# Modulation vectors of a two-layer transformer: sixteen sections as narrow matmuls in four column groups instead of elementwise products with sums

## The chip, the cores and the metric

The kernel runs on one core of a Trainium2 chip. The metric is the device time of one execution in microseconds (us). A core has five engines with their own instruction queues: TensorE (PE in the profile, its weight loads PEld), VectorE (DVE), ScalarE (ACT), GpSimd (POOL) and SyncE (SP), which here issues most of the transfers. They meet only at semaphores.

## What is computed

Two layers over 512 latent and 256 context tokens of 1024 features, in float32. Each layer is a feed-forward block, a mixer and a second feed-forward block, each with a residual and a layer norm; the mixer of layer 0 is a gated linear attention with pooling, that of layer 1 differential attention. Every block's input and residual are modulated by vectors made of two condition vectors, one for the latents and one for the context. The change is in how these are made:

```python
c_act = jax.nn.silu(c)
cc_act = jax.nn.silu(c_ctx)
for layer in range(DEPTH):
    m_lat = jnp.split((c_act @ w_ada[layer] + b_ada[layer])[:, None, :], N_MOD, axis=-1)
    m_ctx = jnp.split(cc_act @ w_ada[layer] + b_ada[layer], N_MOD, axis=-1)
    x = ffn_substep(x, m_lat[0:3], w_ffn_in[layer, 0], ...)
    ...
def ffn_substep(x, mods, w_in, w_out, g, b):
    shift, scale, gate = mods
    y = swiglu(modulate(x, shift, scale), w_in, w_out)
    return layer_norm(ALPHA * x + MACARON * gate * y, g, b)
```

So there are 9 sections of 1024 features a layer, 18 in all, and a section is two row vectors times a matrix of 1024 x 1024 (4 MB).

## The kernel before

Features lie on the 128 partitions in 8 blocks, tokens along the free dimension. Products are made in float32r from a high and a low part (`split`, L115 and L117), with three matmuls for one product (`mm3`, L154 to L156). The order of each engine's instructions is set by the framework's scheduler from the program's order and its own costs, so a piece of code can land among its neighbours.

A feed-forward block, `ffn(l, p)`, makes 22 blocks of the hidden layer (`HB`), each from a block of the gate's weights and one of the value's. The first three blocks (`plain`) are made directly (`project`). The other nineteen, numbers 3 to 21, go by seven products of quarter matrices in place of eight (`seven`): 7 x 4 x 3 = 84 matmuls of 384 columns a block, with weight sums on GpSimd (`ahead`, L645 to L654), seven additions on VectorE (L668) and the hidden values written by `put`. The first 512 tokens' hidden values stay on chip (`G`, in the pool `spare` of eleven tiles); the last 256 tokens' are stored to DRAM (late_g, L561, on the SP queue). Then `out_phase` makes the output product in two halves of the tokens, each over eleven pairs of hidden blocks, and `layer_norm` follows.

The modulation is made in three places. `start` makes the first two sections on TensorE: the conditions are the stationary operand (`ct`, 32 columns a step, two of them used), the weights the moving one, and two column groups of the array take the two halves of 1024 columns side by side, one matmul each (L237). `ada` makes the other sixteen within the first three feed-forward blocks: a step of it is called after every `seven`, for the sections of `in_ada`, and after every step of the output product's first half, for those of `out_ada`. A step loads [128 features x 1024 inputs] of the transposed weights (L174) and multiplies by a condition that was broadcast to all partitions (`load_c`, L167), summing along the row:

```python
for v in vecs:
    if v == LAT or j % 2:
        nc.vector.scalar_tensor_tensor(out=self.tmp("trash").bitcast(BF16), in0=r, scalar=1.0,
                                       in1=self.c_bc[v], op0=ALU.mult, op1=ALU.mult, accum_out=col(v))
    else:
        nc.gpsimd.tensor_mul(out=r, in0=r, in1=self.c_bc[v])
        nc.scalar.activation(out=r, in_=r, func=AF.Copy, accum_out=col(v))
```

That is VectorE's line L183 (its output is the tile "trash") and GpSimd's L186 with ScalarE's L187. Three sections lie in each of these stages of the first and second feed-forward block, (0,0) and (0,1), for both vectors; two in each of the third, (1,0), for the latents alone. `mod[l][v]` holds the results as columns.

## Time and profile before

| | |
|---|---|
| time of one execution, median of 3 runs | 2876.92 us (2876.66 to 2877.67) |
| span of the profiled execution, first to last instruction | 2874.1 us |
| mean granted TensorE clock | 0.983 |
| TensorE busy | 2685.2 us (93%) |
| VectorE busy | 2185.1 us (76%) |
| GpSimd busy | 1074.6 us (37%) |
| ScalarE busy | 1237.0 us (43%) |

The profiled execution is told by its span alone; the times of the runs also hold what lies around the span, and their median is 2.8 us above it. Busy shares are means over stages with different limits, so a stage is read by itself: its length, and which engine has no idle time in it. A busy TensorE is one with a matmul under way, and its ends are modelled; what counts is the distance from one matmul's start to the next.

### The profile page before, as it was taken

The page shows a single profiled execution, that of the slowest core. Times are in us where ns is not written, and L with a number is a line of the kernel's source. Part 1 is how long each engine was busy: PE and PEld are TensorE (multiplying, and loading weights), DVE is VectorE, ACT ScalarE, POOL GpSimd, SP SyncE. Part 2 cuts the span into 40 slices and gives each one's busy share as a digit, 9 for nine tenths or more (in the row PEclk, how much of TensorE's full clock was granted, in tenths as well). Part 3 has the DMA queues.
Part 4 walks back from the last instruction along what each step waited for, and adds up shares of the span by engine and source line. Part 5 has one row for each costly group of instructions (what it writes and reads, how often), then busy time and mean ns, then how long its engine had stood idle before and what let it go on. Part 6 is the DMA issues. An engine that isn't in the chain of part 4 may idle for free.

```text
span 2874.1 us, 44394 instructions
## 1 busy us (share of the span) xinstructions
PE 2685.2 (93%) x17168; PEld 2449.1 (85%) x17168; DVE 2185.1 (76%) x3131; ACT 1237.0 (43%) x1919; POOL 1074.6 (37%) x762
## 2 busy tenths in 40 slices
PE   7889999999999888999999899999999998999997
PEld 4789998887877778989788899998987777999997
DVE  3999978765774689997977888664745887778856
ACT  2333333544543343333345433332534667544444
POOL 0655522241220465643334644410424332366402
PEclk9999999999999999999999999999999999999998
DMA  5343255542114223334555333254541101423454
GB/s 221 111 147 112 105 174 207 195 152 67 56 37 152 88 96 139 118 119 139 206 200 180 110 134 119 82 189 165 184 149 59 41 34 45 158 92 122 155 192 157
DMA packets 139671, 374.24 MB, mean 130 GB/s; under 512 B 16962, under 2 KB 48066, under 8 KB 139460
## 3 DMA queue, kind: packets, MB, share of 16 engines
q1 hardware_dynamic: 136832, 370.21, 37.3%
q8 instruction: 135, 2.21, 0.3%
q10 hardware_dynamic: 2628, 1.20, 0.2%
q14 instruction: 76, 0.62, 0.1%
HBM read 337.78 MB, written 33.56 MB: 129 GB/s over the span
## 4 chain that ended last, share of the span: by engine, by line
PE 58%; DVE 22%; issue 7%; ACT 5%; POOL 4%; DMA 3%; SPq 0%; DVEq 0%; POOLq 0%; ACTq 0%
PE ps L156 17%; PE ps L154 17%; PE ps L155 17%; DVE r4l L117 3%; DVE trash L183 3%; DVE c L668 2%; DVE spare L556 1%; DMA raw<-in_w_ffn_out 1%; PE ps L1187 1%; PE ps L1188 1%; PE ps L1189 1%; DVE sm L1089 1%; DVE b L621 1%; ACT r4h L115 1%; DVE late_g L560 1%
## 5 line engine op out<-in xcount | busy, mean ns | idle before, releaser
L117 DVE TENSOR_TENSOR r4l<-raw,r4h 128x1024 fp32r<-128x1024 f32 (+1 forms) x350 | 449.5, 1286 | 215.5 <-ACT r4h L115 176.3
L154 PE MATMUL ps<-xh,r4h 128*128 128x384 f32 (+2 forms) x1672 | 562.5, 337 | 16.6 <-ACT xh L115 7.0
L155 PE MATMUL ps<-xl,r4h 128*128 128x384 f32 (+2 forms) x1672 | 559.1, 335 | 4.8 <-DVE xl L117 3.2
L156 PE MATMUL ps<-xh,r4l 128*128 128x384 f32 (+2 forms) x1672 | 559.0, 335 | 0.0
L115 ACT CAST r4h<-raw 128x1024 fp32r<-128x1024 f32 (+1 forms) x366 | 358.7, 982 | 443.2 <-PE ps L155 330.7
L156 PE MATMUL ps<-six,r4l 128*128 128x384 f32 (+1 forms) x888 | 294.7, 332 | 69.5 <-DVE r4l L117 69.5
L154 PEld LDWEIGHTS ps<-xh,r4h 128*128 128x128 f32 x1672 | 315.1, 189 | 39.7 <-ACT xh L115 9.5
L155 PEld LDWEIGHTS ps<-xl,r4h 128*128 128x128 f32 x1672 | 315.4, 189 | 24.8 <-DVE xl L117 4.9
L156 PEld LDWEIGHTS ps<-xh,r4l 128*128 128x128 f32 x1672 | 315.4, 189 | 18.1
L668 DVE TENSOR_TENSOR c<-c,ps 128x384 f32<-128x384 f32 (+1 forms) x518 | 261.8, 518 | 49.4 <-PE ps L156 39.5
L154 PE MATMUL ps<-six,r4h 128*128 128x384 f32 (+1 forms) x888 | 292.6, 330 | 0.0
L155 PE MATMUL ps<-six,r4h 128*128 128x384 f32 (+1 forms) x888 | 291.4, 328 | 0.0
L156 PE MATMUL ps<-r4h,r4l 128*128 128x512 f32 (+1 forms) x768 | 278.5, 363 | 13.7 <-DVE r4l L117 13.7
L154 PE MATMUL ps<-r4h 128*128 128x512 f32 (+1 forms) x768 | 278.6, 363 | 0.0
L155 PE MATMUL ps<-r4l,r4h 128*128 128x512 f32 (+1 forms) x768 | 277.3, 361 | 0.0
L156 PE MATMUL ps<-r4h,spare 128*128 128x256 f32 (+1 forms) x896 | 261.0, 292 | 11.5 <-DVE spare L117 11.5
L154 PE MATMUL ps<-r4h,spare 128*128 128x256 f32 (+1 forms) x896 | 263.6, 294 | 1.5 <-ACT spare L115 1.5
L155 PE MATMUL ps<-r4l,spare 128*128 128x256 f32 (+1 forms) x896 | 260.6, 291 | 0.1
L156 PEld LDWEIGHTS ps<-six,r4l 128*128 128x128 f32 x888 | 170.8, 192 | 77.6 <-DVE r4l L117 77.6
L645 POOL TENSOR_TENSOR late<-raw 128x512 f32<-128x512 f32 x74 | 116.6, 1575 | 255.1 <-DMA raw<-in_w_ffn_in 219.2
L654 POOL TENSOR_TENSOR raw<-raw,late 128x512 f32<-128x512 f32 x74 | 98.2, 1327 | 251.3 <-DVE r4l L117 233.8
L156 PEld LDWEIGHTS ps<-r4h,spare 128*128 128x128 f32 x896 | 172.8, 193 | 16.3 <-DVE spare L117 14.2
(292 smaller groups left out, 5969.8 us busy)
## 6 DMA issues: line engine op xcount, KB each, us to landing
raw<-in_w_ffn_in SPq DMA_DIRECT2D x176, 512.0 KB, 4.0
raw<-in_w_ffn_out SPq DMA_DIRECT2D x176, 512.0 KB, 4.2
spare<-in_w_ada SPq DMA_DIRECT2D x80, 512.0 KB, 5.0
six<-in_w_ada SPq DMA_DIRECT2D x64, 512.0 KB, 5.3
g<-late_g SPq DMA_DIRECT2D x88, 128.0 KB, 2.2
raw<-g SPq DMA_DIRECT2D x44, 256.0 KB, 3.3
raw<-in_w_in_even SPq DMA_DIRECT2D x20, 512.0 KB, 3.4
raw<-in_w_in_odd SPq DMA_DIRECT2D x16, 512.0 KB, 3.3
```

The costliest lines, as they stand in the source:

```text
L115: self.copied = self.nc.scalar.copy(out=h, in_=src)
L117: eng.tensor_sub(out=l, in0=src, in1=h.bitcast(F32))
L154: mm(out=ps, lhsT=h, rhs=xh, start=first, stop=False)
L155: mm(out=ps, lhsT=h, rhs=xl, start=False, stop=False)
L156: mm(out=ps, lhsT=l, rhs=xh, start=False, stop=last)
L183: nc.vector.scalar_tensor_tensor(out=self.tmp("trash").bitcast(BF16), in0=r, scalar=1.0, in1=self.c_bc[v], op0=ALU.mult, op1=ALU.mult, acc ...
L556: nc.vector.tensor_mul(out=G(x)[:, 0, a:e], in0=gate[:, :e - a], in1=up[:, :e - a])
L560: nc.vector.tensor_mul(out=t, in0=gate[:, o:b - a], in1=up[:, o:b - a])
L621: sub = lambda o, a, b: nc.vector.tensor_sub(out=o, in0=a, in1=b)
L645: nc.gpsimd.tensor_add(out=s1, in0=a21, in1=a22)
L654: nc.gpsimd.tensor_sub(out=a12, in0=a12, in1=sums[:, 512:])
L668: add = lambda o, a, b: nc.vector.tensor_add(out=o, in0=a, in1=b)
```

## The change

The sixteen sections go to TensorE as well, in pairs. One step takes 128 of the 1024 inputs of both sections: two loads of 512 KB and four matmuls, each of 32 stationary columns (`conditions(k)`, two of them used) and 512 moving ones, for four column groups of the array, whose sums lie in one bank of PSUM on 32 partitions each. After eight steps ScalarE copies the bank, TensorE transposes it in four pieces, and VectorE adds the bias into `mod`. 8 pairs x 8 steps = 64 steps. All of them lie within the seven products of the first three feed-forward blocks, spread over ten calls behind hidden blocks 3 to 12 (24, 24 and 16 steps); the output product has none any more. The weights are loaded in their own order and no longer transposed. The broadcast of the conditions and its copy in DRAM are gone. `ct` is one tile of 46 columns, in which step k's 32 columns begin at 2k, so its transfer writes 64 bytes in one run on each partition, where it wrote 8 runs of 8 bytes. Two small tiles of `_lower_bound` are reused. Docstrings and comments are removed throughout; these lines are left out here.

```diff
-        self.ct = self.tmp("ct")[:, :KB * 32].rearrange("p (k c) -> p k c", k=KB)
+        self.ct = c.tile([P, 2 * KB + 30], F32, name="ct")
         nc.vector.memset(self.ct, 0.0)
-        nc.scalar.dma_start(out=self.ct[:, :, 0:2], in_=ins["ct"])
+        nc.scalar.dma_start(out=self.ct[:, :2 * KB].rearrange("p (k c) -> p k c", k=KB), in_=ins["ct"])
...
-    def load_c(self, tiles):
...
-            nc.sync.dma_start(out=t, in_=(self.ins["c"] if first else self.c_act)[v, :].partition_broadcast(P))
...
-    def ada_load(self, room, l, s, j):
...
-    def ada_block(self, r, l, s, j, vecs):
...
-            if v == LAT or j % 2:
-                nc.vector.scalar_tensor_tensor(out=self.tmp("trash").bitcast(BF16), in0=r, scalar=1.0,
-                                               in1=self.c_bc[v], op0=ALU.mult, op1=ALU.mult, accum_out=col(v))
-            else:
-                nc.gpsimd.tensor_mul(out=r, in0=r, in1=self.c_bc[v])
-                nc.scalar.activation(out=r, in_=r, func=AF.Copy, accum_out=col(v))
...
-    def ada(self, sections, tiles, room, steps):
...
+    def conditions(self, k):
+        return self.ct[:, 2 * k:2 * k + 32]
+
+    def ada(self, sections, room, calls):
+        nc = self.nc
+        pairs = [sections[i:i + 2] for i in range(0, len(sections), 2)]
+        steps = [(q, k) for q in range(len(pairs)) for k in range(KB)]
+        def load(q, k):
+            r = [room() for _ in range(2)]
+            for t, (l, s) in zip(r, pairs[q]):
+                nc.sync.dma_start(out=t, in_=self.ins["w_ada"][l, s, k])
+            return r
+        ahead = [load(*steps[0])]
+        for i, (q, k) in enumerate(steps):
+            if i + 1 < len(steps):
+                ahead.append(load(*steps[i + 1]))
+            if k == 0:
+                ps = self.ps("st")
+            for g, (r, c) in enumerate(itertools.product(ahead.pop(0), range(2))):
+                nc.tensor.matmul(out=ps[32 * g:32 * g + 32, :], lhsT=self.conditions(k), rhs=r[:, c * 512:c * 512 + 512],
+                                 start=k == 0, stop=k == KB - 1)
+            if k == KB - 1:
+                self.ada_finish(pairs[q], ps)
+            if (i + 1) * calls // len(steps) > i * calls // len(steps):
+                yield
+
+    def ada_finish(self, pair, ps):
+        nc = self.nc
+        m = self.tmp("m")
+        nc.scalar.copy(out=m, in_=ps)
+        pt = self.ps()
+        for t in range(4):
+            nc.tensor.transpose(out=pt[:, t * P:(t + 1) * P], in_=m[:, t * P:(t + 1) * P], identity=self.ident)
+        pv = pt.rearrange("p (t i c r) -> p i c t r", t=4, i=2, c=2)
...
+            for v in (LAT, CTX) if l == 0 or s < 5 else (LAT,):
+                o = self.mod[l][v][:, s * KB:(s + 1) * KB]
+                nc.vector.tensor_add(out=view(o), in0=pv[:, i, :, :, v], in1=view(b))
...
@@ start
-        nc.scalar.activation(out=ct, in_=ct, func=AF.Silu)
+        nc.scalar.activation(out=self.ct[:, :2 * KB], in_=self.ct[:, :2 * KB], func=AF.Silu)
...
@@ out_phase
-            if half == 0:
-                with self.behind_weights():
-                    next(ada, None)
...
@@ ffn
-            ada = self.ada(in_ada, [room_of(), room_of()], room_of, HB - 6 - plain) if in_ada else iter(())
+            ada = self.ada(list(ada), room_of, HB - 9 - plain) if ada else iter(())
...
-            both = self.late() if out_ada else None
-            ada = self.ada(out_ada, [both[:, :D], both[:, D:]], lambda: six(F32)[:, :D], HB // 2) if out_ada else iter(())
...
@@ tile_net
-        net.ffn(0, 0, FULL, (0, 3, (LAT, CTX)), (each(0, 2, 5), each(0, 5, 8)), SIGMOID, True)
+        net.ffn(0, 0, FULL, (0, 3, (LAT, CTX)), each(0, 2, 8), SIGMOID, True)
...
-        net.ffn(0, 1, FULL, (1, 0, (LAT, CTX)), (each(0, 8, 9) + each(1, 0, 2), each(1, 2, 5)), SILU)
-        net.ffn(1, 0, FULL, (1, 3, (LAT, CTX)), (each(1, 5, 7), each(1, 7, 9)))
+        net.ffn(0, 1, FULL, (1, 0, (LAT, CTX)), each(0, 8, 9) + each(1, 0, 5), SILU)
+        net.ffn(1, 0, FULL, (1, 3, (LAT, CTX)), each(1, 5, 9))
...
@@ layout
-    r["ct"] = ca(r["c"].reshape(2, KB, P).transpose(2, 1, 0))
+    r["ct"] = ca(np.stack([a["c"][0], a["c_ctx"]]).reshape(2, KB, P).transpose(2, 1, 0))
...
-    r["w_ada"] = ca(a["w_ada"].transpose(0, 2, 1).reshape(DEPTH, N_MOD * KB, P, D))
+    r["w_ada"] = ca(a["w_ada"].reshape(DEPTH, KB, P, N_MOD, D).transpose(0, 3, 1, 2, 4))
```

How the change moves instructions is seen at three places of the first feed-forward block. The first is VectorE within the seven products, around hidden block 4; L668 there is L658 in the new file, L556 and L560 of `put` are L546 and L550, and tile names are those of the program (c for partial products, r4l for the low parts of weights, trash for the discarded output). Before:

```order
L183 SCALAR_TENSOR_TENSOR trash,mod_0_101<-spare 128x1024
L668 TENSOR_TENSOR c<-c,ps 128x384
L183 SCALAR_TENSOR_TENSOR trash,mod_0_101<-spare 128x1024
L556 TENSOR_TENSOR spare<-c 128x128
L560 TENSOR_TENSOR late_g<-c 128x256
L668 TENSOR_TENSOR c<-c,ps 128x384
L183 SCALAR_TENSOR_TENSOR trash,mod_1_102<-spare 128x1024
L556 TENSOR_TENSOR spare<-c 128x384
L117 TENSOR_TENSOR r4l<-raw,r4h 128x1024
L117 TENSOR_TENSOR r4s<-raw,r4s 128x512
L117 TENSOR_TENSOR r4l<-raw,r4h 128x1024
L668 TENSOR_TENSOR c<-c,ps 128x384 x2
```

And now, around block 5:

```order
L658 TENSOR_TENSOR c<-c,ps 128x384 x2
L117 TENSOR_TENSOR r4l<-late,r4h 128x1024
L658 TENSOR_TENSOR c<-c,ps 128x384 x4
L117 TENSOR_TENSOR r4l<-raw,r4h 128x1024
L546 TENSOR_TENSOR spare<-c 128x128
L550 TENSOR_TENSOR late_g<-c 128x256
L658 TENSOR_TENSOR c<-c,ps 128x384
L117 TENSOR_TENSOR r4s<-raw,r4s 128x512
L546 TENSOR_TENSOR spare<-c 128x384
```

The products of 1024 columns between the additions are gone, and the additions follow one another.

The second place is TensorE within block 5. L183 is now the line of the narrow matmuls, and L154 to L156 are the wide ones, of 384 columns:

```order
L156 MATMUL ps<-xh,r4l 128x384
L154 MATMUL ps<-six,r4h 128x384
L183 MATMUL ps<-spare,ct 32x512 x2
L155 MATMUL ps<-six,r4h 128x384
L156 MATMUL ps<-six,r4l 128x384
L154 MATMUL ps<-six,r4h 128x384
L155 MATMUL ps<-six,r4h 128x384
L183 MATMUL ps<-spare,ct 32x512 x2
L156 MATMUL ps<-six,r4l 128x384
L154 MATMUL ps<-six,r4h 128x384
```

A step of four narrow matmuls is split here into two runs of two, with wide ones between them; before, only wide ones stood here. So it is at 15 of the 64 steps, and in all the 256 narrow matmuls stand in 60 runs.

The third place is the end of the modulation behind hidden block 12, first on TensorE (L196 are the transposes):

```order
L155 MATMUL ps<-six,r4h 128x384
L156 MATMUL ps<-six,r4l 128x384
L183 MATMUL ps<-spare,ct 32x512 x8
L196 MATMUL ps<-ident,m 128x128 x4
L154 MATMUL ps<-xh,r4h 128x384
L155 MATMUL ps<-xl,r4h 128x384
```

Two whole steps and then the transposes stand between the products of two hidden blocks, where nothing stood before. On SP the last two loads (L173) stand behind the store of block 12's hidden values (the second late_g):

```order
L551 DMA g_106<-late_g 128x256
L632 DMA raw<-in_w_ffn_in 128x1024
L173 DMA spare<-in_w_ada 128x1024
L632 DMA raw<-in_w_ffn_in 128x1024 x2
L551 DMA g_106<-late_g 128x256
L173 DMA spare<-in_w_ada 128x1024 x2
L632 DMA raw<-in_w_ffn_in 128x1024 x2
L551 DMA g_106<-late_g 128x256
```

Before, at this place, single loads of the modulation alternated with those of the weights.

## Rows read from the trace of the kernel before

**Rows 1.** The page of the profile: busy time, share and instructions of each engine, and the chain that ended last by engine and by line.
```profile
PE 2685.2 (93%) x17168; PEld 2449.1 (85%) x17168; DVE 2185.1 (76%) x3131; ACT 1237.0 (43%) x1919; POOL 1074.6 (37%) x762
...
PE 58%; DVE 22%; issue 7%; ACT 5%; POOL 4%; DMA 3%; SPq 0%; DVEq 0%; POOLq 0%; ACTq 0%
PE ps L156 17%; PE ps L154 17%; PE ps L155 17%; DVE r4l L117 3%; DVE trash L183 3%; DVE c L668 2%; DVE spare L556 1%; DMA raw<-in_w_ffn_out 1%; PE ps L1187 1%; PE ps L1188 1%; PE ps L1189 1%; DVE sm L1089 1%; DVE b L621 1%; ACT r4h L115 1%; DVE late_g L560 1%
```

**Rows 2.** The table by stretches: from and to (us), length, then busy us and instructions of PE, PEld, DVE, ACT and POOL, the mean granted clock, the DMA share and GB/s. The first three rows are the seven products of blocks 3 to 21 in the feed-forward blocks (0,0), (0,1) and (1,0), from the first copy at L670 to the first matmul of the output product; the last three the first half of the output product of the same three, to the first eviction at L431.
```profile
106.00:408.20 302.20, 282.21 (x1567) 278.09 (x1566) 275.22 (x356) 109.08 (x160) 146.18 (x82) 0.99 0.36 127
1057.00:1358.80 301.80, 283.12 (x1567) 278.76 (x1567) 276.45 (x357) 106.89 (x158) 147.29 (x82) 0.98 0.36 127
1631.30:1907.60 276.30, 276.30 (x1566) 276.30 (x1565) 211.06 (x304) 97.90 (x134) 110.88 (x69) 1.00 0.36 124
408.20:531.90 123.70, 116.80 (x503) 94.78 (x502) 104.82 (x118) 52.70 (x73) 33.35 (x12) 0.99 0.60 205
1358.80:1482.40 123.60, 116.76 (x502) 94.76 (x501) 104.07 (x120) 45.65 (x57) 33.40 (x12) 0.99 0.58 203
1907.60:2020.40 112.80, 112.80 (x500) 93.39 (x499) 58.19 (x74) 33.00 (x33) 0.00 (x0) 1.00 0.53 185
```

**Rows 3.** The timeline of ACT at the start of the program: start, length, engine, line, operation, and in brackets the idle time before it and what ended it. L230 is the activation of the conditions, L240 the copy of the first columns.
```profile
11.22 0.42 ACT L230 ACTIVATE ct<-ct 128x256 f32<-128x256 f32 x1 [6.82 <-DMA ct<-in_ct]
...
20.34 0.58 ACT L240 COPY m<-ps 64x512 f32<-64x512 f32 x1 [7.19 <-PE ps L237]
```

**Rows 4.** DMA issues of the whole program: tile and source, issuing queue, count, KB of each, median us from issue to landing.
```profile
spare<-in_w_ada SPq DMA_DIRECT2D x80, 512.0 KB, 5.0
...
late<-c_act SPq DMA_DIRECT2D x6, 512.0 KB, 7.2
...
ln<-in_ln ACTq DMA_DIRECT2D x1, 48.0 KB, 3.9
...
ct<-in_ct ACTq DMA_DIRECT2D x1, 8.0 KB, 10.0
```

**Rows 5.** Timelines of ACT, PE and DVE around the three marks of block (0,0): the first copy of a product, the first matmul of the output product (L154), the first eviction (L431).
```profile
105.97 0.47 ACT L670 COPY c<-ps 128x384 f32<-128x384 f32 x1
...
408.18 0.39 PE L154 MATMUL ps<-r4h 128*128 128x512 f32 x1
...
531.91 0.48 DVE L431 SCALAR_TENSOR_TENSOR six<-ps,mod,six 128x256 f32<-128x256 f32 x1
```

**Rows 6.** Groups by line and shape: the modulation's instructions on VectorE and GpSimd. Busy us and mean ns of one, then idle time before them and what ended it.
```profile
L183 DVE SCALAR_TENSOR_TENSOR trash<-spare 128x1024 bf16<-128x1024 f32 x88 | 151.9, 1726 | 0.0
...
L183 DVE SCALAR_TENSOR_TENSOR trash<-six,late 128x1024 bf16<-128x1024 f32 x88 | 125.2, 1453 | 25.9 <-DMA six<-in_w_ada 25.8
...
L186 POOL TENSOR_TENSOR six<-six,late 128x1024 f32<-128x1024 f32 x24 | 70.3, 2928 | 193.7 <-DVE trash L183 167.8 <-DMA six<-in_w_ada 10.5 <-ACT r4h L115 8.5
...
L186 POOL TENSOR_TENSOR spare<-spare 128x1024 f32<-128x1024 f32 x24 | 64.4, 2682 | 48.9 <-DVE trash L183 41.0 <-PE ps L156 7.9
```

**Rows 7.** The timeline of ACT in block (1,0), where no modulation is left to make. L670 is the copy of a block's first product, and comes once a block.
```profile
1863.31 0.62 ACT L115 CAST r4s<-raw 128x512 fp32r<-128x512 f32 x1 [0.87 <-PE ps L155]
1863.84 1.05 ACT L115 CAST r4h<-raw 128x1024 fp32r<-128x1024 f32 x1
1865.60 0.48 ACT L670 COPY c<-ps 128x384 f32<-128x384 f32 x1 [0.72 <-PE ps L156]
...
1880.40 0.48 ACT L670 COPY c<-ps 128x384 f32<-128x384 f32 x1 [0.72 <-PE ps L156]
```

**Rows 8.** The table by stretches for the start of the program, columns as in rows 2.
```profile
2.00:14.00 12.00, 2.31 (x6) 0.55 (x8) 1.27 (x9) 3.19 (x4) 0.00 (x0) 1.00 0.90 321
14.00:36.00 22.00, 18.66 (x89) 11.86 (x86) 11.72 (x21) 7.65 (x9) 0.00 (x0) 0.92 1.02 399
```

**Rows 9.** The timeline of PE at the start of the program. L237 are the narrow matmuls of the first modulation, two column groups side by side, eight steps in a run; L243 the transposes after them.
```profile
11.69 8.60 PE L237 MATMUL ps<-spare,ct 128*32 128x512 f32 x32 [11.69 <-DMA spare<-in_w_ada]
21.07 0.43 PE L243 MATMUL ps<-ident,m 64*128 64x64 f32 x4 [0.77 <-ACT m L240]
...
38.31 0.28 PE L154 MATMUL ps<-xh,r4h 128*128 128x256 f32 x1
38.42 0.29 PE L155 MATMUL ps<-xl,r4h 128*128 128x256 f32 x1
38.55 0.27 PE L156 MATMUL ps<-xh,r4l 128*128 128x256 f32 x1
38.75 7.06 PE L237 MATMUL ps<-spare,ct 128*32 128x512 f32 x32
45.74 0.50 PE L154 MATMUL ps<-xh,r4h 128*128 128x512 f32 x1
```

**Rows 10.** The timeline of PE's weight loads within the first run of L237: each row is two loads, one for each column group, for one pass.
```profile
15.41 0.11 PEld L237 LDWEIGHTS ps<-spare,ct 128*32 128x32 f32 x2 [0.32 <-issue]
15.84 0.11 PEld L237 LDWEIGHTS ps<-spare,ct 128*32 128x32 f32 x2 [0.32 <-issue]
```

**Rows 11.** The timeline of PE in the even mixer: matmuls of 32 columns in four column groups side by side (24 matmuls, 48 records a row).
```profile
684.23 0.72 PE L816 MATMUL ps<-late,km 128*32 128x32 f32 x48
684.76 0.64 PE L816 MATMUL ps<-q,t 128*32 128x32 f32 x48
```

**Rows 12.** The timeline of the SP queue in block (1,0), where no modulation is left to make: the store of a hidden block's later tokens (g).
```profile
1863.58 0.33 SPq L561 DMA_DIRECT2D g<-late_g  x1
```

More of the change, by code (lines that the diff above doesn't have):

```diff
@@ L236, in columns @@
                 for s in range(2):
[L237 removed]
+                    nc.tensor.matmul(out=ps[32 * s:32 * s + 32, :], lhsT=self.conditions(k), rhs=r[:, s * 512:s * 512 + 512],
                                      start=k == 0, stop=k == KB - 1)
@@ L359, in table, with out_phase @@
             self.nc.scalar.preload_act_table_set(name)
-    def out_phase(self, pool, nk, wsrc, gsplit, halves, gate, l, i, nxt, r_of, table=None, keep=False, ada=iter(())):
+    def out_phase(self, pool, nk, wsrc, gsplit, halves, gate, l, i, nxt, r_of, table=None, keep=False):
         nc = self.nc
@@ L528, in project, with ffn @@
                 done(x, h)
-    def ffn(self, l, p, halves, nxt, ada=((), ()), table=None, first_of_all=False):
+    def ffn(self, l, p, halves, nxt, ada=(), table=None, first_of_all=False):
         nc, tc, ins = self.nc, self.tc, self.ins
@@ L1215, in _lower_bound @@
         nc = self.nc
-        e, s, lb, om = (pool.tile([P, 8], F32, name=f"lb{i}") for i in range(4))
+        e, s = (pool.tile([P, 8], F32, name=f"lb{i}") for i in range(2))
+        lb, om = s, e
         nc.vector.tensor_sub(out=e, in0=x, in1=x)
```

48 lines of the change are left out of this document (8 added, 40 removed).

## The prediction

> **What bounds the kernel now.** The totals come first [rows 1]: TensorE is busy for 93% of the span and VectorE for 76%, and the chain that ended last lies on TensorE for 58% of the span and on VectorE for 22%, with the modulation's own line (trash, L183) at 3.0%. That is a mean over stages, so the next view is the table by stretches [rows 2]. It sets three feed-forward blocks side by side: for each, the stretch of the seven products (blocks 3 to 21, from the first copy of a product to the first output product) and the first half of the output product (to the first eviction). The three do the same products on the same shapes; they differ in how much modulation lies within them. In the third block, where only the latent vectors are made, TensorE is busy for all of 276.3 us and all of 112.8 us. In the first two VectorE is busy for 275 of 302 us and TensorE has some 20 us of idle time, and 7 us in the output half. So in two blocks VectorE sets the pace, and in the third TensorE does, with no idle time to fill. The start, last, is set by neither engine: TensorE's first weights wait for the activation of the conditions, and that for its transfer [rows 3], which took 10.0 us for 8 KB [rows 4]. The marks of the first block's two stretches are [rows 5].
>
> **What it removes.** (a) 176 VectorE products of 1024 columns of 1.45 to 1.73 us and 48 GpSimd ones of 2.7 to 2.9 us [rows 6], with the ScalarE sums behind these. Their worth is not their 277 us of VectorE time but what the first two blocks are longer than the third: 302.2 - 276.3 = 25.9 and 301.8 - 276.3 = 25.5 us in the seven products, and 123.7 - 112.8 = 10.9 and 123.6 - 112.8 = 10.8 us in the output half [rows 2]. Sum 73.1 us. The third block gives nothing. Blocks without modulation on VectorE go by at 14.80 us each [rows 7], which I take as the pace of all of them.
> (b) At the start the conditions come as one run of 64 bytes per partition in place of eight of 8 bytes. The other small loads beside it show what that is worth: 48 KB in one run per partition landed in 3.9 us [rows 4]. The activation now ends at 11.64 [rows 3]; with a landing like that one's it would end near 5.5, so at most some 6.5 us go, and none if the transfers that follow set the pace anyway. These move 321 GB/s between 2 and 14 us and 399 GB/s after it [rows 8]: 12 us x (399 - 321) / 399 = 2.3 us are lost there. I take 4 us, between the two; the eight first steps (8.60 us [rows 9]) then end when their weights land.
>
> **What it adds, all of it on TensorE.** (c) 64 steps of four matmuls [32 columns of conditions x 512] in float32, each two records. Two column groups side by side take one pass per 0.43 us [rows 10], so 0.86 us for a step, and eight steps took 6.99 us from start to start of what follows [rows 9]. Whether four go as fast as two is shown only for short ones: 48 records of 32 columns in four groups started within 0.53 us [rows 11], where one after the other, at 0.43 / 512 x 32 = 27 ns each, they would take 1.3 us. So at least 2.5 lie abreast there, and 11 ns between two starts looks like a limit of issue, which eight records in 0.86 us do not meet. I take four abreast: 0.86 us a step; at 2.5 abreast it would be 1.37. The order on TensorE (shown with the change) adds to this: 15 of the 64 steps are split into two runs of two matmuls with wide products between, and a run of two costs what a run of four does. 49 + 30 = 79 runs' worth x 0.858 = 67.8 us.
> The Trainium skill, page "TensorE: Matmul & The Clock Gate", section "Measured speedup vs the span model", has three column groups of 512 columns at 2.38 times one, 0.79 of what full overlap would give; by an estimate from that figure the 49 whole steps would cost 0.23 us more each, 11 us in all. No run here shows four long ones, so it stays inside the range.
> (d) Going from wide products to narrow ones and back. Before the eight steps at 38.75 the products of 256 columns start 0.12 us apart; the narrow ones start 0.20 after the last, and 6.99 us later the next, against 8 x 0.858 = 6.86 [rows 9]. That is 0.08 + 0.13, about 0.2 us for a run; 60 runs stand in the order, 12.0 us.
> (e) Eight times a copy and four transposes, which the order puts right behind a pair's last step, so that TensorE stands while ScalarE copies: from the end of the matmuls to the transposes it took 0.77 us at the start [rows 9], the copy being 0.58 of it [rows 3], and four transposes 0.43. In the seven products the copy stands behind two casts of 0.62 and 1.05 us that run just then [rows 7]. I take 1.5 us with the transposes; 1.2 and 2.6 are the ends. 8 x 1.5 = 12.0 us. The small adds that follow on VectorE have the time that its products gave up.
> (f) Waits for weights. SP is one queue, and the loads of the modulation stand in it behind the store of the hidden block just made. In the steady pace that store is issued 0.3 us after the block's last product (the r4s cast at 1863.31 starts with the next block's products, the store is at 1863.58) [rows 7, 12], and a load lands a median 5.0 us later [rows 4]. A split step comes some 5.4 us into the next block (one whole step, then 24 products of 14.80 / 84 us), so its loads are just there. The last step of the first and second feed-forward block is asked for 1 us after block 12, and lands at 0.3 + 0.45 + 5.0: 4.8 us of stall, twice, 9.6 us. Ends 4 and 14.
>
> **The sum.** -73.1 - 4.0 + 67.8 + 12.0 + 12.0 + 9.6 = +24.3 us. The profiled span of 2874.1 becomes 2898.4; the median of the three runs, 2876.9, lies 2.8 above that span, and with the same distance the time is **2901.2 us**. By blocks: start -4, first -36.8 + 39.4, second -36.3 + 39.4, third +22.5: in the first two narrow work on TensorE eats the whole relief of VectorE, and the third pays for it outright.
>
> **The rivals.**
> Not slower: narrow matmuls run beside the wide ones at their borders, so that a split half costs only its own 0.43 us and a change of width nothing. Place: the 60 runs; price: 15 x 0.858 + 12.0 = 24.9 us less, 2876.3 us. It decides if a run of two costs the wide products less than 0.5 us. Against it stand the two borders in [rows 9]. 7 in 100.
> Two groups at a time: the short matmuls of [rows 11] do not carry over, and 49 whole steps cost 1.4 to 1.7 us. +26 to +42: 2927 to 2943 us. For it: only 2.5 abreast is proven. 10 in 100.
> Late weights: the loads stand in groups of six to ten on SP, and if a landing takes 7.2 us, as that of the broadcast conditions does in the same stages [rows 4], the 15 split steps stall, by up to 2.2 us each, and the two last stalls grow as much. With some 10 of the 17 hit, 20 us more: 2921 us. For it: TensorE now waits in order for transfers that VectorE alone waited for. 15 in 100.
> My forecast holds the other 68, with -10 to +20 for its own terms (start 0 to 6.5, transposes and stalls between their ends, a border 0.1 to 0.25).
>
> **The numbers.** A range of 2876 to 2926 takes in the forecast's own 2891 to 2921, the late weights and the first rival's edge, and leaves out the two-at-a-time case and the far end. A change of 0.2%, 5.8 us, is about what a measurement here can tell from none. Faster by more than that needs the first rival and a start at its upper bound: 0.05. Within it, the first rival alone or all of my costs at their low ends: 0.07. Slower: 0.88.
>
> **What would show it.** Right: VectorE falls to some 200 us in each of the three stretches, as in the third now; the seven products of the first two take about 316 us and their output halves 113; the third's takes 299; the narrow matmuls' groups keep 0.86 us a step; TensorE is idle for some 5 us behind block 12 of the first two; TensorE's first record stands near 6 us. Wrong: a step of four at 1.4 us or more, a half step at half the time, transposes that wait for nothing, or a third block under 285 us.

## The result, and the profile after

The changed kernel took 2919.69 us (median of four runs, 2911.16 to 2932.85) beside 2877.30 for the kernel before in the same comparison: a ratio of 1.015, interval 1.012 to 1.018. It is slower by 42 us; forecast was 24 us slower, 2901.2, in a range of 2876 to 2926. Direction and range held. The size did not, and the likeliest case of the four was not the one that came. A second comparison, below, has the change at +35 us (2919.7 beside 2884.7): the changed kernel came out the same both times and the kernel before did not, so the miss is 11 to 18 us. The profiled execution is the slowest of the four runs (2932.85, span 2931.0), so sums below are made against it and then held against a second profile and against medians.

The page's totals and its chain, which answer to [rows 1]:

```profile
PE 2771.3 (95%) x17712; PEld 2460.8 (84%) x17712; DVE 1833.6 (63%) x2775; ACT 1196.9 (41%) x1829; POOL 911.1 (31%) x714
...
PE 32%; DVE 6%; ACT 2%; issue 2%; DMA 1%; POOL 1%; SPq 0%; POOLq 0%; ACTq 0%; DVEq 0%
```

VectorE lost 352 us of work. The chain here reaches back over only part of the span (its shares add up to 44%), so they are not to be set against those of before. The table by stretches does better. These are the stretches of [rows 2] with the same columns: the seven products of the three feed-forward blocks, then their output halves.

```profile
105.50:429.70 324.20, 314.45 (x1771) 281.88 (x1770) 185.97 (x293) 106.23 (x151) 103.37 (x69) 0.98 0.43 154
1070.80:1397.90 327.10, 316.70 (x1770) 283.58 (x1769) 183.89 (x297) 100.21 (x137) 104.15 (x69) 0.98 0.43 153
1660.60:1962.90 302.30, 298.21 (x1703) 278.54 (x1703) 181.69 (x277) 99.72 (x136) 103.02 (x69) 0.99 0.40 138
429.70:542.50 112.80, 112.80 (x499) 93.39 (x499) 40.32 (x38) 34.17 (x35) 0.00 (x0) 1.00 0.29 100
1397.90:1510.70 112.80, 112.80 (x500) 93.39 (x499) 40.03 (x37) 33.13 (x33) 0.00 (x0) 1.00 0.30 100
1962.90:2075.70 112.80, 112.80 (x499) 93.39 (x499) 40.04 (x38) 33.12 (x33) 0.00 (x0) 1.00 0.30 101
```

Read the length first. The output halves are 112.8 us, all three, as forecast (113). The seven products were forecast at 316, 316 and 299 and came at 324, 327 and 302. Next read PE's busy time against the length: some 10 us of each of the first two are idle, 4 us of the third. VectorE is at 182 to 186 us, so it is not the bound anywhere here.

What TensorE does in there, in its timeline (columns: start, length, operation, idle time before and what ended it). A record is one pass, so x8 is a whole step and x4 a half:

```profile
115.75 2.78 PE L183 MATMUL ps<-spare,ct 128*32 128x512 f32 x24
...
133.31 1.07 PE L183 MATMUL ps<-spare,ct 128*32 128x512 f32 x8
139.16 1.05 PE L183 MATMUL ps<-spare,ct 128*32 128x512 f32 x4 [0.17 <-DMA spare<-in_w_ada]
...
213.94 1.05 PE L183 MATMUL ps<-spare,ct 128*32 128x512 f32 x4 [1.66 <-DMA spare<-in_w_ada]
215.82 1.05 PE L183 MATMUL ps<-spare,ct 128*32 128x512 f32 x4
...
284.99 1.07 PE L183 MATMUL ps<-spare,ct 128*32 128x512 f32 x8
290.18 1.92 PE L183 MATMUL ps<-spare,ct 128*32 128x512 f32 x4 [4.12 <-DMA spare<-in_w_ada]
292.28 1.92 PE L183 MATMUL ps<-spare,ct 128*32 128x512 f32 x4 [0.18 <-DMA spare<-in_w_ada]
294.95 1.11 PE L196 MATMUL ps<-ident,m 128*128 128x128 f32 x4 [0.74 <-ACT m L193]
295.71 0.67 PE L154 MATMUL ps<-xh,r4h 128*128 128x384 f32 x1
296.18 0.52 PE L155 MATMUL ps<-xl,r4h 128*128 128x384 f32 x1
...
299.03 0.34 PE L156 MATMUL ps<-xh,r4l 128*128 128x384 f32 x1
```

Three things stand in these rows. A whole step (1.07) and a half (1.05) cost the same; three steps in a run take 2.78, so a further step is 0.86. Halves wait for their own load, up to 1.66 us. And behind block 12 the last step waits 4.12 us and then runs at half speed: its halves take 1.92 us each and the wide products 0.52, until they are back at 0.34 near 299. The granted clock of these two stretches is in the table by stretches (the value ahead of the DMA share):

```profile
285.00:295.70 10.70, 5.66 (x21) 1.28 (x21) 1.79 (x4) 2.13 (x3) 2.00 (x2) 0.66 0.58 209
295.70:299.50 3.80, 3.80 (x16) 3.80 (x15) 1.82 (x10) 0.10 (x1) 1.76 (x2) 0.62 0.00 0
299.50:309.70 10.20, 10.20 (x61) 10.20 (x60) 4.95 (x7) 3.02 (x4) 1.30 (x1) 1.00 0.01 2
```

0.66 and 0.62 are means of the two levels, 2.4 and 1.2 GHz. SP's queue at that place, where L551 is the store of the hidden block and L173 the last step's two loads:

```profile
285.27 0.33 SPq L551 DMA_DIRECT2D g<-late_g  x1
285.69 0.94 SPq L173 DMA_DIRECT2D spare<-in_w_ada  x2
```

The page's rows of DMA issues for the conditions and for the modulation's loads, which answer to [rows 4] (the last value is the median us to landing):

```profile
ct<-in_ct ACTq DMA_DIRECT2D x1, 8.0 KB, 4.8
spare<-in_w_ada SPq DMA_DIRECT2D x144, 512.0 KB, 7.1
```

The request comes where and when it was predicted. The halves of the last step start 4.5 and 6.6 us after it, and over the program the median landing is 7.1 us, with two loads in a row, where the kernel before had 5.0, with one at a time. That the pairing alone makes the difference was not tried.

### The profile page after: what moved, and what is told of

Its sections match the earlier page's. It is cut to its first block, busy times and chain, and to the rows that moved or that the text cites. A ratio compares the mean times of both kernels' runs of the same rounds, so it can differ in the third digit from the quotient of the medians.

```text
span 2931.0 us, 45010 instructions
## 1 busy us (share of the span) xinstructions
PE 2771.3 (95%) x17712; PEld 2460.8 (84%) x17712; DVE 1833.6 (63%) x2775; ACT 1196.9 (41%) x1829; POOL 911.1 (31%) x714
## 5 line engine op out<-in xcount | busy, mean ns | idle before, releaser
L117 DVE TENSOR_TENSOR r4l<-raw,r4h 128x1024 fp32r<-128x1024 f32 (+1 forms) x350 | 419.4, 1200 | 495.6 <-ACT r4h L115 341.4
L154 PE MATMUL ps<-xh,r4h 128*128 128x384 f32 (+2 forms) x1672 | 570.5, 342 | 18.0 <-DVE K L1022 11.4
L156 PE MATMUL ps<-xh,r4l 128*128 128x384 f32 (+2 forms) x1672 | 562.5, 337 | 0.4 <-DVE r4l L117 0.4
L154 PEld LDWEIGHTS ps<-xh,r4h 128*128 128x128 f32 x1672 | 318.9, 191 | 65.1 <-issue 19.5
L658 DVE TENSOR_TENSOR c<-c,ps 128x384 f32<-128x384 f32 (+1 forms) x518 | 262.0, 519 | 139.8 <-PE ps L156 133.7
L155 PEld LDWEIGHTS ps<-xl,r4h 128*128 128x128 f32 x1672 | 319.0, 191 | 24.7 <-DVE xl L117 4.5
L156 PEld LDWEIGHTS ps<-xh,r4l 128*128 128x128 f32 x1672 | 318.7, 191 | 22.4 <-issue 3.4
L156 PE MATMUL ps<-six,r4l 128*128 128x384 f32 (+1 forms) x888 | 291.2, 328 | 32.7 <-DVE r4l L117 32.7
L154 PE MATMUL ps<-six,r4h 128*128 128x384 f32 (+1 forms) x888 | 289.1, 326 | 0.0
L154 PE MATMUL ps<-r4h 128*128 128x512 f32 (+1 forms) x768 | 277.5, 361 | 0.0
L156 PE MATMUL ps<-r4h,r4l 128*128 128x512 f32 (+1 forms) x768 | 276.1, 360 | 0.2 <-DVE r4l L117 0.2
L156 PE MATMUL ps<-r4h,spare 128*128 128x256 f32 (+1 forms) x896 | 261.2, 292 | 11.9 <-DVE spare L117 11.7
L154 PE MATMUL ps<-r4h,spare 128*128 128x256 f32 (+1 forms) x896 | 263.4, 294 | 1.5 <-ACT spare L115 1.5
L635 POOL TENSOR_TENSOR late<-raw 128x512 f32<-128x512 f32 x74 | 109.6, 1480 | 483.8 <-DMA raw<-in_w_ffn_in 406.7
L156 PEld LDWEIGHTS ps<-six,r4l 128*128 128x128 f32 x888 | 169.3, 191 | 43.7 <-DVE r4l L117 33.6
L156 PEld LDWEIGHTS ps<-r4h,spare 128*128 128x128 f32 x896 | 172.9, 193 | 16.7 <-DVE spare L117 14.6
L644 POOL TENSOR_TENSOR raw<-raw,late 128x512 f32<-128x512 f32 x74 | 105.9, 1431 | 236.3 <-DVE r4l L117 215.7
```

Source lines behind the costliest of these rows:

```text
L117: eng.tensor_sub(out=l, in0=src, in1=h.bitcast(F32))
L154: mm(out=ps, lhsT=h, rhs=xh, start=first, stop=False)
L155: mm(out=ps, lhsT=h, rhs=xl, start=False, stop=False)
L156: mm(out=ps, lhsT=l, rhs=xh, start=False, stop=last)
L635: nc.gpsimd.tensor_add(out=s1, in0=a21, in1=a22)
L644: nc.gpsimd.tensor_sub(out=a12, in0=a12, in1=sums[:, 512:])
```

## The experiments

Two theories stood first. **L**: what the forecast missed are late weights on TensorE, with the lower clock behind them. **P**: the matmuls and their borders cost more than was taken. Every ratio is to the kernel before, timed beside the variant on the same chip. That kernel itself took 2883.5 to 2884.7 us on the three chips used there, against 2877.3 for the first comparison. So the variants are set against the second timing of the changed kernel, r_after, by their medians. One reservation goes with all of these differences: the first copy of a product stands at 104.4 us in the profile of r_after and at 99 to 101 in those of the variants of the changed kernel (102.7 without the sections), though these edits are to later stages. Up to 5 us of a difference can come from there; the last section says why.

**The changed kernel again.** No edit.

> The changed kernel itself, again, beside its variants. Its first four runs spread over 22 us (2911 to 2933), where the kernel before spreads over 4. If the spread comes from waits of TensorE for weights and the lower clock behind them (theory L), this run shows it again: 2911 to 2933, with waits of 4 us or more for the modulation's weights behind block 12 of the first two blocks. If the first profile was an odd one (theory O), the five runs lie within 5 us of one another.

Measured: 2919.7 us (2917.8 to 2925.1), ratio 1.013 (1.0112 to 1.0148). Its profile has 320.1, 327.7 and 300.9 us for the seven products, and four waits of TensorE for modulation weights in the second block, 8.5 us in all, the longest 4.4. The waits recur; the first block has one of 4.0 us behind block 12. The spread here was 7 us, neither the 22 of theory L nor under the 5 of theory O, so the spread proves nothing for L.

**Loads asked for earlier.**

```
-        ahead = [load(*steps[0])]
+        ahead = [load(*s) for s in steps[:2]]
         for i, (q, k) in enumerate(steps):
-            if i + 1 < len(steps):
-                ahead.append(load(*steps[i + 1]))
 ...             # the four matmuls of step i
+            if i + 2 < len(steps):
+                ahead.append(load(*steps[i + 2]))
```

> The changed kernel with each step's two loads asked for right behind the step two before it, and so ahead of a hidden block's border and not behind it; same tiles, same matmuls, 44 runs in place of 61. Theory L (late weights and the half clock behind them are what was missed): the two stalls behind block 12, 7 us each, and the slower clock behind them, 3.4 us each, go, the split steps fall from 15 to 4 at 1.2 us each and their waits with them: 30 to 40 us less, 2880 to 2890. Rival P (the price of the matmuls and their borders is what was missed, the stalls being hidden in part): only the 11 splits go, 13 us less, 2905. Rival Q (the loads only collide earlier with those of the feed-forward weights): no change or slower, 2915 to 2930.

Measured: 2883.9 us (2880.0 to 2891.9), ratio 0.9998 (0.9987 to 1.0009): 36 us less. The whole loss against the kernel before is gone. Its stretches of the seven products:

```profile
100.40:407.60 307.20, 303.98 (x1771) 280.89 (x1770) 184.76 (x293) 106.50 (x152) 104.06 (x69) 1.00 0.47 163
1047.10:1354.00 306.90, 303.33 (x1770) 280.24 (x1769) 181.92 (x296) 100.12 (x137) 102.26 (x69) 1.00 0.46 163
1616.00:1911.20 295.20, 293.16 (x1703) 278.54 (x1702) 184.03 (x277) 99.33 (x136) 104.16 (x69) 1.00 0.41 141
```

The granted clock is 1.00 in all three, and what TensorE still waits for is mostly the copy ahead of the transposes. The waits of TensorE in the first stretch (us in total, times, longest), of the changed kernel:

```profile
PE ps L183 <- DMA spare<-in_w_ada: 7.1, 6, 4.1
PE ps L196 <- ACT m L193: 2.6, 3, 1.0
```

The same of this one, where L181 are the narrow matmuls:

```profile
PE ps L196 <- ACT m L193: 2.8, 3, 1.0
PE ps L181 <- DMA spare<-in_w_ada: 0.4, 1, 0.4
```

L is upheld, P falls (it gave 2905), and Q, that earlier loads would only collide, falls too. The landing is still 6.5 us there: the loads are hardly faster, their waits are covered. The 36 us are not the waits alone: the same edit leaves 4 split steps of the 15, which P priced at 13 us, and the two were not tried apart. The three stretches together are 39 us shorter than those of r_after.

**Transposes one block later.** `ada_finish` becomes a generator, and `ada` resumes it a call later.

```
 # ada
             if k == KB - 1:
-                self.ada_finish(pairs[q], ps)
+                later = self.ada_finish(pairs[q], ps)
+                next(later)
             if (i + 1) * calls // len(steps) > i * calls // len(steps):
                 yield
+                next(later, None)
 ...
 # ada_finish
         nc.scalar.copy(out=m, in_=ps)
+        yield
         pt = self.ps()
```

> The changed kernel with the four transposes of a pair one hidden block later than the copy that they read, so that TensorE need not stand while ScalarE copies. By the trace a pair's end costs some 1.6 us on TensorE, of which 0.42 are the transposes and 0.2 their borders: 8 x 1.0 = 8 us less, 2912. Rival: the copy's time was hidden by loads that are late anyway (no pair's next step is loaded when the copy ends), so 0 to 3 us less.

Measured: 2904.5 us (2899.0 to 2910.9), ratio 1.0075 (1.0057 to 1.0092): 15 us less, about twice what was expected. The first two stretches took 315.3 and 313.6 us, against 320.1 and 327.7. By the trace their time in narrow runs and transposes, beyond 0.858 us a step, fell from 22.4 and 27.7 us to 16.3 and 15.6. Three copies a block at 1.0 us do not account for that, and the halves are no fewer (14 against 12). The start also came 4 us earlier in this profile (100.0 against 104.4), which the edit does not touch. So 8 us can be the copies, and whether the other 7 come from the start or from the halves stays open.

**Whole steps.**

```
-            for g, (r, c) in enumerate(...):
+            for g, (r, c) in reversed(list(enumerate(...))):
```

> The changed kernel with the four matmuls of a step in the reverse order, so that the first of them waits for the load that comes last: the order on TensorE then has no split step (51 runs of whole steps, where there were 61 with 30 halves). If a half run costs what a whole one does (0.98 against 1.00 us in the trace, plus 0.1 to 0.2 at its head): 15 x 1.1 = 16 us less, 2903. Rival (a half's cost is covered, since the other half waits for its weights in any case): within 4 us of the changed kernel.

Measured: 2907.1 us (2905.3 to 2909.1), ratio 1.0084 (1.0069 to 1.0099): 13 us less. A half run is no half price, and the rival falls. The waits are still there, the longest now 6.7 and 6.2 us, since the whole step waits for the later of its two loads; the two long stretches took 317.6 and 317.0 us, with the mean granted clock at 0.98.

**The idle time filled.**

```
+            if i == len(steps) - 1 and len(pairs) == 3:
+                fill = self.ps()
+                for _ in range(18):
+                    nc.tensor.matmul(out=fill, lhsT=self.xh[:, 0, :P], rhs=self.xh[:, 0, :512], start=True, stop=True)
             for g, (r, c) in enumerate(...):
```

> The changed kernel with 18 matmuls more (128x512, into a bank that nobody reads, some 4 us) ahead of the last step of the first and second block, where TensorE waits 4 us for weights and then runs at the lower clock for 8 us. It adds work and takes no wait away. Theory (the lower clock there follows from the idle time, and costs 3.4 us a time): the steps behind take 1.0 us in place of 2, the wide matmuls 0.175 and not 0.32, and the first two stretches get shorter by 3 us each, 2913. Rival (the clock falls there for another reason): the extra work hides in the wait and nothing else moves, 2920; or, where the wait was shorter than 4 us, some us slower.

TensorE's timeline at the same place as above, where L187 are the narrow matmuls, L185 those that fill, L200 the transposes:

```profile
277.66 1.06 PE L187 MATMUL ps<-spare,ct 128*32 128x512 f32 x8
278.65 4.42 PE L185 MATMUL ps<-xh 128*128 128x512 f32 x18
283.21 1.05 PE L187 MATMUL ps<-spare,ct 128*32 128x512 f32 x4
285.48 1.05 PE L187 MATMUL ps<-spare,ct 128*32 128x512 f32 x4 [1.21 <-DMA spare<-in_w_ada]
287.27 0.65 PE L200 MATMUL ps<-ident,m 128*128 128x128 f32 x4 [0.74 <-ACT m L197]
```

With work in the wait, the halves take 1.05 us, not 1.92, and the granted clock of both first stretches is 1.00 in place of 0.98. So the lower clock there follows from the idle time: shown by the rows. Measured: 2914.2 us (2904.4 to 2915.7), ratio 1.0101 (1.0084 to 1.0118). The 5.5 us are in the expected direction, but their intervals overlap and the first copy stands 5.3 us earlier than in r_after (99.1), so the time alone shows nothing. The expected 3 us in each of the first two stretches did not come evenly: 321.2 and 320.2 us, against 320.1 and 327.7 in r_after and 324.2 and 327.1 in the first profile. The clock is also a small part of the stall: the second half still waits 1.21 us for its weights, and from the step ahead of the stall to the transposes it is 9.61 us here and was 9.96.

**Nothing of the sixteen sections.** The modulation's columns are set to zero at the start, and:

```
-        net.ffn(0, 0, ..., each(0, 2, 8), SIGMOID, True)
+        net.ffn(0, 0, ..., (), SIGMOID, True)
 ...                    # and so for (0, 1) and (1, 0)
```

> The changed kernel without the sixteen sections: their loads, matmuls, transposes and adds are left out and the modulation's columns are zero, so it computes something else; its time is that of the rest. It bounds what the modulation costs in either form. Theory (the relief is what the first two blocks were longer than the third, 73 us, and the start gives up to 4): 73 to 77 us less than the kernel before, that is 2801 to 2805 where that one takes 2878, and the three stretches of the seven products at 276 us each. Rival (VectorE has other work at the same places, so part of the 73 us stays): 50 to 60 us less.

Measured: 2799.9 us (2796.7 to 2802.4) beside 2883.5, ratio 0.9709 (0.969 to 0.9729): 84 us less. Its table by stretches, the seven products and the first two output halves:

```profile
102.70:379.10 276.40, 276.40 (x1567) 276.40 (x1566) 180.06 (x269) 104.87 (x149) 103.89 (x69) 0.99 0.30 93
1023.90:1300.40 276.50, 276.50 (x1567) 276.50 (x1566) 176.21 (x268) 98.60 (x134) 103.95 (x69) 0.99 0.29 93
1562.50:1837.80 275.30, 275.30 (x1567) 275.30 (x1567) 179.14 (x269) 98.67 (x134) 104.17 (x69) 1.00 0.30 94
379.10:491.80 112.70, 112.70 (x499) 93.29 (x498) 39.93 (x36) 34.28 (x35) 0.00 (x0) 1.00 0.32 101
1300.40:1413.30 112.90, 112.90 (x499) 93.47 (x499) 40.12 (x38) 33.23 (x33) 0.00 (x0) 1.00 0.32 101
```

Without modulation all blocks go at the third's pace, so the relief was read rightly from the difference between stretches. The six stretches together are 73.8 us shorter than those of [rows 2] (1240.4 against 1166.6). The 7 to 11 us beyond the expectation are not shown in the profile: it is 73.6 us shorter than that of the kernel before (2800.5 against 2874.1), with 3.3 us won at the first copy and 3.6 lost in the stages between the stretches. The kernel before took 6 us more here than in the first comparison, so the rest stays open. The work that the change adds is 2919.7 - 2799.9 = 120 us by medians, and 120.5 by the seven products of the two profiles; the forecast had 101.4.

**The contiguous conditions alone.** The kernel before with this part of the change (and `_lower_bound`'s tiles used again, for room):

```
-        self.ct = self.tmp("ct")[:, :KB * 32].rearrange("p (k c) -> p k c", k=KB)
+        self.ct = c.tile([P, 2 * KB + 30], F32, name="ct")
-        nc.scalar.dma_start(out=self.ct[:, :, 0:2], in_=ins["ct"])
+        nc.scalar.dma_start(out=self.ct[:, :2 * KB]..., in_=ins["ct"])
...
-                    ... lhsT=ct[:, k, :] ...
+                    ... lhsT=ct[:, 2 * k:2 * k + 32] ...
```

> The kernel before with the conditions in one contiguous tile alone, as the change has it. Theory as predicted: TensorE's first record 5 us earlier, 4 us left of it at the end of the first steps, and 4 us less in all. Rival (the trace of the changed kernel): the lead shrinks to 0.4 us by the first copy of a product, since TensorE runs at the lower clock behind the wait at 50 us; then 0 to 1 us less, which no measurement here can tell from nothing.

Measured: 2873.7 us (2869.6 to 2878.2), ratio 0.9971 (0.996 to 0.9981): 10 us less, more than either theory gave. In its profile the first copy of a product stands at 97.7 us, against 106.0: 8.3 us earlier. The rival, which I had drawn from one profile of the changed kernel, falls. The section on the hardware shows where the start's gain comes and goes.

**The third block back on VectorE.** `ada_v` is the kernel before's `ada`, with its `load_c` and its call in the output product:

```
-        net.ffn(1, 0, FULL, ..., each(1, 5, 9))
+        net.ffn(1, 0, FULL, ..., (), (each(1, 5, 7), each(1, 7, 9)))    # ada_v: seven products, output product
```

> The changed kernel with the four sections of block (1,0) back on VectorE, two within the seven products and two within the output product, as in the kernel before. Theory (the third block pays for TensorE's work outright and gets nothing for it, since VectorE had idle time there): its seven products return from 302 to 276 us, the output half stays at 113, and 26 us go: 2894 beside 2920 for the changed kernel. Rival (VectorE is fuller there than it looked, since the two loads and the hidden layer's casts share its queue): 10 us or less.

Measured: 2888.6 us (2883.3 to 2898.1), ratio 1.0022 (1.001 to 1.0033): 31 us less. The third block's two stretches:

```profile
1647.90:1923.40 275.50, 275.50 (x1566) 275.50 (x1565) 211.90 (x302) 100.12 (x136) 114.29 (x69) 1.00 0.37 124
1923.40:2036.20 112.80, 112.80 (x500) 93.38 (x499) 59.16 (x75) 33.14 (x33) 0.00 (x0) 1.00 0.54 185
```

VectorE takes 30 us of modulation here without making the stretch longer. 25 of the 31 us are in it (300.9 in r_after to 275.5), and the first copy stands 5 us earlier (99.3).

**The three mendings together, and versions that beat both kernels.** e7 has the three edits; e8 adds the third block on VectorE; e9 moves four more sections to VectorE, in the first output half of their blocks:

```
-  each(0, 2, 8), ((), ())                    ...  each(0, 8, 9) + each(1, 0, 5), ((), ())
+  each(0, 2, 6), ((), each(0, 6, 8))         ...  each(0, 8, 9) + each(1, 0, 3), ((), each(1, 3, 5))
```

> The changed kernel with the earlier loads, the transposes one block later and the reverse order of a step's matmuls together: 40 runs of whole steps. Alone they gave 36, 15 and 13 us. If they are separate costs that add up: 64 us less, 2856. If they overlap, as theory L has it (the second and third lie in the waits and splits that the first takes away, but for eight copies at 1.0 us and four splits at 1.1): 36 + 8 + 4 = 48 us less, 2872.

Measured: 2871.6 us (2866.7 to 2873.2), ratio 0.9959 (0.9945 to 0.9973): 48 us less than the changed kernel, as theory L had it. The second and third mending overlap with the first.

> The changed kernel with all three mendings (earlier loads, transposes one block later, whole steps) and with the four sections of block (1,0) on VectorE, as in the kernel before. With the mendings the third block's seven products still take 292 us where 276 are enough: 16 us less than with the mendings alone, 2855. Rival (the clock or the loads take it back, as 26 us of the trace became 31 us in that experiment with the third block alone): anything between 2845 and 2865.

Measured: 2847.0 us (2844.3 to 2848.6), ratio 0.9875 (0.986 to 0.9889). Faster than the kernel before by 36 us. Against e7 that is 25 us less where 16 were expected, within the rival's range: 17 of them are in the third stretch, which fell from 292.3 to 275.3, and the other 8 were not traced to a cause.

> As the one before, and two of the six sections of each of the first two blocks on VectorE within the output product's first half, where VectorE is busy for 40 of 113 us without modulation and three sections brought it to 105 and the half to 124 us. A pair fewer on TensorE saves 9 us a block (27 to 28 us for three pairs in the mended kernel); two sections are 43 us on VectorE, 83 of 113, and should cost 0 to 4 us: 10 to 18 us less, 2841. Rival (VectorE bounds the output half by its place in the chain and not by its sum): the half goes to 120 and the gain to 4 us or less.

Measured: 2844.9 us (2840.0 to 2846.0), ratio 0.9863 (0.9845 to 0.988), not told apart from e8: the 10 to 18 us that were expected did not come, and the gain of 2 us has the rival's size. Its first two stretches and their output halves:

```profile
100.70:393.00 292.30, 292.30 (x1703) 277.84 (x1703) 183.68 (x285) 99.44 (x136) 104.50 (x69) 1.00 0.42 142
1039.00:1331.40 292.40, 292.40 (x1702) 277.94 (x1702) 183.56 (x287) 99.52 (x136) 105.16 (x70) 1.00 0.41 142
393.00:513.00 120.00, 115.83 (x502) 94.89 (x501) 86.36 (x96) 50.88 (x67) 25.56 (x8) 0.99 0.50 175
1331.40:1446.60 115.20, 113.90 (x502) 93.96 (x502) 83.92 (x97) 41.42 (x49) 22.53 (x8) 1.00 0.54 183
```

Against e8 a pair fewer gave 11.3 and 12.5 us back in the seven products, and the output halves took 7.3 and 2.4 of them. VectorE is busy for 86 and 84 us there, so the forecast's slack of 30 us was not all to be had. Of the other 14 us, 10 went again in the stages behind the third block's output half, 860.4 against 850.1 us; both kernels have the same work there, and why they differ was not tried.

## Why the forecast was right in direction and short in size

**The relief (-73.1): right.** The output halves fell to 112.8 as read, and without any modulation the seven products take 276.4 and 276.5; the six stretches are 73.8 us shorter in that profile.

**The start (-4.0, ends 0 and -6.5): mis-sized.** TensorE's first record stands at 6.24, near the 6 that was forecast; the conditions' load landed in 4.8 us. The gain of this alone was 10 us by medians and 8.3 at the first copy, beyond my upper end. In the changed kernel's first profile only 0.5 us of it was left at the first copy of a product (105.5 against 106.0), in its second 1.6. I had bounded the term by the transfers and not looked at what stands behind it, TensorE's wait of 2.5 us for VectorE at 51 us.

**A step (0.86) and a half step (the same): right.** 0.86 for a further step in a run, 1.07 for one alone, 1.05 for a half. Four column groups of 512 columns lie fully abreast, and the two-at-a-time rival falls. The Trainium skill, page "TensorE: Matmul & The Clock Gate", section "Measured speedup vs the span model", has three groups at 2.38 times one; by an estimate from it, 0.79 of full overlap, that is 11 us more here. The trace does not agree: 0.86 us a step is two passes of 0.43, with no loss.

**The borders (0.2 each): right.** The rows give 0.09 us ahead of a run and 1.00 - 0.86 = 0.14 within and behind it, 0.23. Steps and borders come to 49 x 0.855 + 32 x 0.235 for the whole ones and 30 x 1.07 for the halves, 81.5 us; forecast 79.8. (The trace has 62 runs, two more than the order's groups, where transposes part them.) The rival that narrow matmuls run beside the wide ones falls.

**The transposes (1.5 a pair): right** on TensorE. From the end of a step to the next wide product stand 0.79 to 1.02 us of waiting and 0.41 to 0.59 of transposes at the full clock.

**The waits for weights (9.6 us): this step failed.** "Its loads are just there" was wrong, and so was the size of the last stall. The two last steps cost 7.0 and 7.3 us more than a whole step should, where I had 4.8. Most of it is the second of the two loads: the last half starts 6.6 and 6.9 us after the request, that is 6.4 and 6.7 us later than behind a whole step. The lower clock, which I did not have at all, is the small part: with the idle time filled, at the full clock, the two places still cost 6.7 and 6.3. The split halves and the pieces between took another 10.4 us, where I had none; 7.5 of these stand in the trace as eight waits for weights. (Narrow runs, transposes and their borders took 45.9, 47.0 and 25.3 us in the three stretches, 118.2; less 81.5 and 12.0 that is 24.7.) Together 15.1 us more than forecast. The duration that failed is the landing: 5.0 us of [rows 4] was that of single loads among others; the change asks for two at once, and they land in 7.1 (why was not tried). The late-weights rival had put 7.2 us there and named the mechanism. That its 2921 us is what came (2919.7) is in part luck: it had 20 us more in late weights, where 15 were found, and terms that it did not have made up the rest.

**What is left.** The wide products of the three stretches took 6.4 us more than three times the third stretch of before would have; some of it is the half clock behind the two stalls (about 1.3 us on the nine wide products behind the first). The stages between the marks took 5.9 us more in the first profile than before, 1533.6 against 1527.6 us. The change has no edit there, and the kernel before with the contiguous conditions alone had 1531.7; over all profiles these stages lie between 1524 and 1536. So I count the 5.9 to the run, which is argued and not shown. The sum against the first profile: 15.1 (waits) + 6.4 + 1.7 (steps and borders) + 3.5 (start) + 5.9 = 32.6, which is 56.9 - 24.3. The second profile has the same terms, most of them smaller: 12.8 + 3.9 + 1.7 + 2.4 + 4.2 = 25.0, where 49.2 - 24.3 is 24.9. Both sums are larger than the miss by medians, 11 to 18 us, since the profiled runs of the changed kernel are its slowest and that of the kernel before is a fast one.

**The third block: right.** It paid outright, 302 where 299 was forecast, and returns to 275.5 when its sections go back.

## What to carry to other kernels

Work that moved from a parallel engine into TensorE's own order was paid in full here in the stage that TensorE bounded. Leave it on the other engine there: one stretch of this kernel took 30 us of it on VectorE without getting longer. Where an engine waits in order for weights, look at what stands in front of their loads in the queue, and price the landing from loads that are asked for in the same way, here two at once; asking one step earlier, ahead of a block's border, with the same tiles, was worth 36 us here, more than any other single edit.

## What the runs showed of the hardware that was not expected

**Part of the start's gain hangs on a collision of VectorE and GpSimd.** VectorE scales the input (L269) while GpSimd makes the first sums of weights (L645 to L647). The timelines of the two in the kernel before:

```profile
47.66 3.92 DVE L269 TENSOR_SCALAR spare<-spare,mod 128x512 f32<-128x512 f32 x5
51.50 2.88 DVE L117 TENSOR_TENSOR xl<-spare,xh 128x768 fp32r<-128x768 f32 x2
...
48.60 1.40 POOL L645 TENSOR_TENSOR late<-raw 128x512 f32<-128x512 f32 x1 [47.30 <-DMA raw<-in_w_ffn_in]
```

And with the contiguous conditions alone:

```profile
42.41 1.97 DVE L269 TENSOR_SCALAR spare<-spare,mod 128x512 f32<-128x512 f32 x5
44.29 1.82 DVE L117 TENSOR_TENSOR xl<-spare,xh 128x768 fp32r<-128x768 f32 x2
...
44.52 2.75 POOL L645 TENSOR_TENSOR late<-raw 128x512 f32<-128x512 f32 x1 [43.21 <-DMA raw<-in_w_ffn_in]
```

Where GpSimd comes in 0.9 us after VectorE's first product, the two take turns of some 1.4 us, the five products take 3.92 us in place of 1.97, and TensorE waits 2.5 us for xl. Where it comes 1.7 us after or later, it is GpSimd that waits (2.75 us for one sum of 1.4), and TensorE does not wait at all. In all 13 profiles the wait goes by that distance: 0.90 to 0.98 us gave 2.5 us (six), 1.24 to 1.54 gave 0.5 (three), 1.66 to 2.22 gave none (four). In three of the six with the long wait, both profiles of the changed kernel among them, the granted clock behind it was 0.50 for a while; in the other three it was 1.00. The first copy of a product follows: from the first of the five products to it are 55.3 to 55.7 us without the wait, 56.6 to 56.7 with the short one, 58.1 to 58.3 with the long one at the full clock and 59.6 to 61.4 with the long one and the lower clock. That makes up most of the 4 to 5 us by which the two profiles of the changed kernel start later than those of its variants. That the two engines keep each other waiting agrees with the Trainium skill, page "Trainium Architecture — The Big Picture", section "What this means for kernel authors", by which the pair shares a port to SBUF that one of them holds at a time; which of the two waits, by the distance between them, is what these profiles show. An edit that moved GpSimd alone was not tried.

**A wait of 4 us cost the clock as well.** Behind the waits of 4.1 and 4.2 us of the changed kernel the granted clock fell to the lower level; with the wait filled by other matmuls it did not. By these rows it cost some 2.5 us behind the first of the two, an estimate: 0.9 on the last half, 0.3 on the transposes and 1.3 on nine wide products. How long the lower clock lasts differs at the same place: in the first block of r_after the wait was 4.0 us, the granted clock 0.50 for the 3.2 us of the step, and the wide products were back at 0.34 at once.

```profile
287.43 3.20 PE L183 MATMUL ps<-spare,ct 128*32 128x512 f32 x8 [4.00 <-DMA spare<-in_w_ada]
291.78 0.42 PE L154 MATMUL ps<-xh,r4h 128*128 128x384 f32 x1
292.05 0.34 PE L155 MATMUL ps<-xl,r4h 128*128 128x384 f32 x1
```

Shorter waits than 4 us were followed by it too, but not always: of the six waits of 2.5 us at the start, three.
